# First weight differences of the second feed-forward block queued behind the last norm and the last sum; its operands transposed in another order

## The chip, the cores and the metric

One core of one Trainium2 chip runs the whole kernel. The metric is the device time of one execution in microseconds (us); a kernel's time is the median of its runs. Engines are named as in the profile: PE (TensorE matmuls), PEld (its weight loads), DVE (VectorE), ACT (ScalarE), POOL (GpSimd), SP (SyncE, whose queue issues the loads and stores).

## What is computed

One decoder layer on 1024 tokens of width 1024, in float32: a gated feed-forward half-step, a mixing stage (two kinds of attention, merged by gates), a second feed-forward half-step, and a gated per-layer embedding. The change lies where the mixing stage ends and the second feed-forward begins:

```python
def rms_norm(x, g):
    xf = x.astype(jnp.float32)
    r = lax.rsqrt(jnp.mean(xf * xf, axis=-1, keepdims=True) + NORM_EPS)
    return (xf * r).astype(x.dtype) * g

def swiglu(u, w_in, w_out):                      # w_in: 1024 x 5632, w_out: 2816 x 1024
    a, b = jnp.split(u @ w_in, 2, axis=-1)
    return (jax.nn.silu(a) * b) @ w_out
...
        h = h + merged @ w_out[i]
        h = h + FFN_RES_WEIGHT * swiglu(rms_norm(h, ffn2_norm[i]), ffn2_w_in[i], ffn2_w_out[i])
```

## The kernel before

**Products.** Each float32 operand is split into a high part (a cast to fp32r on ACT) and a low part (operand minus high part, on DVE or POOL); a product takes three matmuls, high by high, high by low, low by high.

**Tokens.** The residual stream h lies as eight tiles of 128 tokens, t = 0 to 7. `chunked` ends the mixing stage: for each t it adds the last product to h (two halves, line 256, DVE) and calls `after2(t)`, which stores h to DRAM, normalises it (`normed`: squares and their sum on ACT, line 303; the scale r on POOL, lines 201 and 202; h times r times the gain on DVE, line 305) and, for t from 4 on, calls `left.sums`.

**Seven products for eight.** The up-projection of the feed-forward works on a 2 by 2 block scheme with seven products per column block f of 128 hidden channels (22 blocks). Its left operands are seven sets, made from the normalised tokens: a11, a12 and a22 are quarters of them, s1 to s4 sums and differences of quarters, which `Left.sums` computes on POOL: for each of four token tiles the lines 330 (s1), 331 (s3), 333 (s2) and 334 (s4). `Left.put(name)` makes a set usable: for each of four tiles, four transposes on PE into one PSUM bank (line 187), a cast on ACT (line 211), a subtraction on DVE (line 212). A product (line 407) is 12 matmuls of 512 columns over all four tiles of one set. Its second matmul already reads low parts, so it needs the last tile's subtraction.

**Weights.** `load_a(f)` loads and splits the first weight tile (line 364, then 368 on ACT and 369 on POOL). `load_t(f)` loads the second, makes four differences on DVE (lines 384 to 387, two SBUF inputs each) and splits them: lines 368 (ACT) and 369 (POOL), twice for 128x1024 of differences and once for 128x512 of the raw tile ("wb"). A raw buffer is one of three; the next load into it waits for line 387 or for the splits.

**Order.** `Up.run` interleaves the first two column blocks: products 1 of block 0, 1 of block 1, 2 and 2, and then 5, 6, 7, 3, 4 of block 0 and the same of block 1. In `A_OF`, product 1 uses a11, 2 a12, 5 s1, 6 s2, 7 s3, 3 s4, 4 a22. After the n-th product one set of the list `puts` is put, and a hook for n is called: here `load_t(0)` at n = 1 and `load_t(1)` at n = 5. PE executes in the order of the code; the other engines' queues are ordered by a scheduler at build time, which may move instructions ahead of where the code has them. Every queue then runs strictly in that order.

Of the kernel before, what the change touches and what calls it, by code (L numbers as in the profile page):

```python
# [16 lines left out]
ALU = mybir.AluOpType  # L17
# [29 lines left out]
def hybrid_layer_kernel(  # L47
# [6 lines left out]
    nc = tc.nc  # L54
# [115 lines left out]
    def defer(ns, key, fn):  # L170
        later.append((pe["t"] + ns, key, fn))
        later.sort(key=lambda e: e[0])

    def need(key):

        mine = [e for e in later if e[1] == key]
        for e in mine:
            later.remove(e)
        for e in mine:
            e[2]()  # L180
# [14 lines left out]
    def rsqrt_mean(ss, n, cols=1, add=None):  # L195
        r = small.tile([P, 8], F32, tag="r", name="r")
        if add is not None:
            nc.gpsimd.tensor_scalar(r[:, :cols], ss, add, 1.0 / n, op0=ALU.add, op1=ALU.mult)
            nc.gpsimd.tensor_scalar(r[:, :cols], r[:, :cols], EPS, None, op0=ALU.add)
        else:  # L200
            nc.gpsimd.tensor_scalar(r[:, :cols], ss, 1.0 / n, EPS, op0=ALU.mult, op1=ALU.add)  # L201
        nc.gpsimd.tensor_tensor(r[:, :cols], r[:, :cols], mhalf[:, :cols], op=ALU.pow)
        return r

    def bcast_row(pool, v, n):
        g = pool.tile([P, n], F32, tag="gbc", name="gbc", bufs=1)
        nc.sync.dma_start(out=g[:, :n], in_=v.partition_broadcast(P))
        return g
# [92 lines left out]
    def normed(un, squares, src, g):  # L301
        ss = small.tile([P, 8], F32, tag="ss", name="ss")
        nc.scalar.activation(squares, src, AF.Square, accum_out=ss[:, 0:1])
        r = rsqrt_mean(ss[:, 0:1], DM)
        nc.vector.scalar_tensor_tensor(un, src, r[:, 0:1], g, op0=ALU.mult, op1=ALU.mult)

    class Left:

# [16 lines left out]
        def sums(self, t, part=(0, 1)):  # L325
            x11, x12 = self.un0[:, t, :512], self.un0[:, t, 512:]
            x21, x22 = self.un1[:, t, :512], self.un1[:, t, 512:]
            s1 = self.s1(t)
            if 0 in part:
                nc.gpsimd.tensor_add(s1, x21, x22)  # L330
                nc.gpsimd.tensor_sub(x21, x11, x21)
            if 1 in part:
                nc.gpsimd.tensor_sub(x11, s1, x11)
                nc.gpsimd.tensor_sub(self.s4(t), x12, x11)

        def put(self, name, ts=range(4)):
            pss = []
# [12 lines left out]
    class Up:  # L350
# [122 lines left out]
        def run(self, left, puts, late, hooks):  # L473

            two = [self.block(f, left) for f in range(2)]
            seq = [(0, 1), (1, 1), (0, 2), (1, 2)] + [(b, i) for b in range(2) for i in (5, 6, 7, 3, 4)]
            hooks = hooks | {6: lambda: self.load_a(2), 9: lambda: self.load_t(2)}
            for n, (b, i) in enumerate(seq):
                two[b][i]()
                if puts:  # L480
                    left.put(puts.pop(0))
                if n in hooks:
                    hooks[n]()
            for f in range(2, NF):
                b = self.block(f, left)
                b[1]()
                if f + 1 < NF:
                    self.load_a(f + 1)
                    self.load_t(f + 1)
                else:  # L490
                    late()
                for i in (6, 2, 5, 7, 3, 4) if f + 1 == NF else (6, 5, 2, 7, 3, 4):
                    b[i]()

    class Down:
# [73 lines left out]
        def run(self, scale, open_raws, open_norm, h_of, after):  # L569
# [36 lines left out]
            for n, (k, i) in enumerate(self.steps):  # L606
# [14 lines left out]
                if i == self.N - 1:  # L621
                    for j, ps in enumerate(pss.pop(k)):
# [7 lines left out]
    up = Up(ffn1_w_in, hs_d)  # L630
# [8 lines left out]
    left1 = Left(un0, un1, lambda t: s1_[t], lambda t: un0[:, t, 512:],  # L639
                 dict(a11=(upool, "u"), a12=(upool, "u"), a22=(upool, "u"), s3=(upool, "u"),  # L640
                      s1=(ux, "ux"), s2=(ux, "ux"), s4=(ux, "ux")))
# [41 lines left out]
    for t0 in range(0, NT, 2):  # L683
# [3 lines left out]
        r = rsqrt_mean(ss[:, :2], DM, 2)  # L687
# [7 lines left out]
    for c in range(2):  # L695
        col = slice(c * 512, (c + 1) * 512)
        for t in range(NT):
# [7 lines left out]
            n = c * NT + t  # L705
# [12 lines left out]
        for i in range(2):  # L718
            down.load(1, i, nc.gpsimd)

    up.run(left1, ["s1", "s2", "a22", "s3", "s4"], early, {1: open1, 4: lambda: up.load_t(1)})
    st_f.close()
    st_u.close()

    def run_down(down, name, h_src, gain, spill):

        st_h, st_n, st_r, st = (ExitStack() for _ in range(4))
        hp = phase(st_h, "h" + name, 1, "right")
        u, box = [], {}

        def open_raws(d):
            d.raws = phase(st_r, "raws" + name, 4, "right")
            d.more = phase(st, "dmore" + name, 1)
            d.temps = phase(st, "temps" + name)

        def h_of():
            h = box["h"] = hp.tile([P, NT, DM], F32, name="h")
            for t in range(NT):
                nc.sync.dma_start(out=h[:, t, :], in_=h_src[t * P:(t + 1) * P, :])
            return h  # L740

        def open_norm():
            st_r.close()
            box["n"] = phase(st_n, "norm" + name, 1, "right")
            box["g"] = bcast_row(box["n"], gain, DM)

        def after(t):
            if t % 4 == 0:
                u.append(new_u())
            norm_tile(box["n"], u, box["h"], t, box["g"], 7000.0 + 3200.0 * (t % 4))  # L750
            if spill:
                nc.sync.dma_start(out=h_spill[t * P:(t + 1) * P, :], in_=box["h"][:, t, :])

        down.run(0.5, open_raws, open_norm, h_of, after)
        st.close()
        return box["h"], u, (st_n, st_h)

    h, um, st_h = run_down(down, "1", x, mix_norm, True)
# [53 lines left out]
    left = [16 * 48 * 216.0]  # L812
# [189 lines left out]
    for t in range(NT):  # L1002
# [15 lines left out]
        r = rsqrt_mean(ss, QK, H)  # L1018
# [23 lines left out]
    for t in range(NT):  # L1042
# [15 lines left out]
        r = rsqrt_mean(ss, QK, H, add=sskr[:, t:t + 1])  # L1058
# [216 lines left out]
    h = hp.tile([P, NT, DM], F32, name="h2")  # L1275
# [24 lines left out]
        return hid  # L1300

    up = Up(ffn2_w_in, hs_d)
    left2 = []

    def ahead():
        up.load_a(0)
# [6 lines left out]
    def after2(t):  # L1313
        nc.sync.dma_start(out=h_spill[t * P:(t + 1) * P, :], in_=h[:, t, :])
        left = left2[0]
        un = (left.un0 if t < 4 else left.un1)[:, t % 4]
        normed(un, un, h[:, t, :], g2)
        if t < 4:
            defer(9500.0, "a11", lambda: left.put("a11", [t]))
        else:  # L1320
            if t == 5:
                need("a11")
                left.sums(0, (1,))
            left.sums(t - 4, (0,) if t == 4 else (0, 1))

    g2 = bcast_row(mp, ffn2_norm, DM)
    chunked(h, KT, (lambda ct: branch_w(w_branch_mla, ct), merge_up), w_out, 1.0, ahead,
            tuple(range(NT)), after2)
    need("a11")
    st.close()  # L1330
# [10 lines left out]
    def early2():  # L1341
        for i in range(2):
            down.load(1, i, nc.gpsimd)

    up.run(left2[0], ["a12", "s1", "s2", "s3", "s4", "a22"], early2,
           {1: lambda: up.load_t(0), 5: lambda: up.load_t(1)})
    st_f.close()
    st_u.close()
    h, u3, st_h = run_down(down, "2", h_spill, ple_norm, False)
# [4 lines left out]
    for c in range(2):  # L1354
        col = slice(c * 512, (c + 1) * 512)
        dg = [w_rows(w_ple_gate, 2 * j * P, c * 512, 512, 2) for j in range(4)]
        for half in range(2):
            need((id(u3), half))
            pss, pps = [bank() for _ in range(4)], []
            for k0 in (0, 4):  # L1360
                for j in range(4):
                    t, tc0 = 4 * half + j, j * P
# [47 lines left out]
```

## Time and profile before

| | |
|---|---|
| time, median of 3 runs (lowest, highest) | 2375.73 us (2372.26, 2380.26) |
| the profiled execution: its time, its span | 2373.98 us, 2371.9 us |
| PE busy | 2292.8 us, 97% of the span |
| DVE busy | 1525.5 us, 64% |
| ACT busy | 956.2 us, 40% |
| POOL busy | 852.1 us, 36% |
| chain that ended last, PE's share | 79% |

The busy share of an engine is an average over the span. PE is at work nearly all the time, so time can be lost or won where PE waits. The time of the profiled execution is 2.1 us longer than its span. Times below are us from the span's start.

### The profile page before, as it was taken

The numbers are of one execution on the slowest core, as the hardware profiler recorded it, in microseconds if no ns is written. First come the engines' busy times: TensorE is split into PE (matmuls) and PEld (weight loads), VectorE is DVE, ScalarE is ACT, GpSimd is POOL, SyncE is SP. The second block draws the span as 40 slices with busy tenths as digits, with TensorE's granted clock in tenths as the row PEclk, the third lists the DMA queues.
The fourth block names the chain that finished last, engine by engine and source line by source line (L and its number), as shares of the span: only waits on it lengthen the run. The fifth ranks groups of instructions, "written<-read, shape, count | busy, mean of one in ns | idle before, by whom it ended". The sixth has DMA issues, their size and how long they took to land.

```text
span 2371.9 us, 30099 instructions
## 1 busy us (share of the span) xinstructions
PE 2292.8 (97%) x11160; PEld 1912.0 (81%) x11160; DVE 1525.5 (64%) x2001; ACT 956.2 (40%) x1604; POOL 852.1 (36%) x654
## 2 busy tenths in 40 slices
PE   7899999999999999899999998998999999999999
PEld 6788888878888988777777887887888888888887
DVE  7667676657772224577777778557776666677842
ACT  5333233325452233455556666224233233244441
POOL 7444444400032233442333542547444444300030
PEclk9999999999999999999999999999999999999999
DMA  6223233385555324885453566512233332585432
GB/s 230 85 89 111 89 111 95 119 322 180 186 174 150 96 85 116 234 219 107 101 104 96 148 180 197 188 63 80 88 122 94 110 111 89 200 287 187 139 133 80
DMA packets 293890, 331.85 MB, mean 140 GB/s; under 512 B 16624, under 2 KB 200176, under 8 KB 293744
## 3 DMA queue, kind: packets, MB, share of 16 engines
q1 hardware_dynamic: 269808, 296.38, 39.0%
q0 software_dynamic: 23936, 33.56, 6.8%
q8 instruction: 87, 1.43, 0.2%
q14 instruction: 59, 0.48, 0.1%
HBM read 230.79 MB, written 99.09 MB: 139 GB/s over the span
## 4 chain that ended last, share of the span: by engine, by line
PE 79%; DVE 7%; DMA 5%; POOL 4%; issue 2%; ACT 2%; SPq 0%; DVEq 0%; ACTq 0%; POOLq 0%
PE T L183 37%; PE T L407 34%; PE A L183 5%; PE T L187 4%; DMA raw<-in_ffn_w_out_dram 2%; DVE D L1162 1%; POOL D L143 1%; DMA k_d<-ev 1%; DVE p L1162 1%; DVE D L1163 1%; DVE pt L212 1%; POOL D L369 1%; POOL hid L263 0%; DVE op L1112 0%; DMA un<-in_x_dram 0%
## 5 line engine op out<-in xcount | busy, mean ns | idle before, releaser
L407 PE MATMUL T<-u,D 128*128 128x512 f32 x3168 | 733.3, 391 | 3.6 <-DVE u L430 2.4
L407 PEld LDWEIGHTS T<-u,D 128*128 128x128 f32 x3168 | 596.0, 189 | 129.3 <-DVE u L430 4.1
L183 PE MATMUL T<-D 128*128 128x512 f32 x1944 | 452.4, 393 | 5.9 <-DVE u L212 2.3
L183 PEld LDWEIGHTS T<-D 128*128 128x128 f32 x1944 | 366.2, 189 | 83.5 <-ACT D L532 3.2
L369 POOL TENSOR_TENSOR D<-ts,D 128x1024 fp32r<-128x1024 f32 x88 | 216.5, 2460 | 309.9 <-ACT D L368 309.8
L183 PE MATMUL T<-u,D 128*128 128x512 f32 x1152 | 288.2, 396 | 11.1 <-DVE op L1112 11.1
L143 POOL TENSOR_TENSOR D<-raw,D 128x256 fp32r<-128x256 f32 (+6 forms) x159 | 188.4, 1211 | 292.2 <-ACT D L139 269.4
L183 PEld LDWEIGHTS T<-u,D 128*128 128x128 f32 x1152 | 209.2, 188 | 55.0 <-DVE op L1112 16.2
L532 ACT CAST D<-raw 128x512 fp32r<-128x512 f32 (+1 forms) x154 | 123.7, 807 | 225.2 <-PE T L183 113.7
L368 ACT CAST D<-ts 128x1024 fp32r<-128x1024 f32 x88 | 92.5, 1051 | 289.7 <-PE T L407 273.2
L201 POOL TENSOR_SCALAR r<-ss 128x1 f32<-128x1 f32 (+2 forms) x52 | 17.4, 335 | 497.7 <-ACT un L221 404.2
L183 PE MATMUL T<-D,u 128*128 128x512 f32 (+2 forms) x960 | 195.9, 362 | 0.0
L183 PEld LDWEIGHTS T<-D,u 128*128 128x128 f32 x960 | 166.2, 188 | 21.8
L533 DVE TENSOR_TENSOR D<-raw,D 128x512 fp32r<-128x512 f32 (+1 forms) x146 | 131.1, 900 | 60.3 <-ACT D L532 59.3
L212 DVE TENSOR_TENSOR pt<-T,pt 128x512 fp32r<-128x512 f32 (+1 forms) x160 | 101.1, 634 | 72.7 <-ACT pt L211 71.2
L369 POOL TENSOR_TENSOR D<-raw,D 128x1024 fp32r<-128x1024 f32 x44 | 121.2, 2756 | 34.1 <-ACT D L368 34.1
L407 PE MATMUL T<-u,wb 128*128 128x512 f32 x528 | 126.8, 389 | 0.0
L211 ACT CAST pt<-T 128x512 fp32r<-128x512 f32 (+1 forms) x160 | 86.7, 544 | 90.1 <-PE T L187 88.2
L384 DVE TENSOR_TENSOR ts<-raw 128x512 f32<-128x512 f32 x44 | 36.0, 818 | 134.6 <-POOL D L369 130.0
L407 PEld LDWEIGHTS T<-u,wb 128*128 128x128 f32 x528 | 99.1, 188 | 20.6
L385 DVE TENSOR_TENSOR ts<-raw,ts 128x512 f32<-128x512 f32 x44 | 114.1, 2594 | 0.0
L450 DVE TENSOR_TENSOR hidf<-u,sg 128x512 f32<-128x512 f32 x44 | 105.3, 2394 | 9.9 <-ACT sg L448 9.4
(224 smaller groups left out, 3311.6 us busy)
## 6 DMA issues: line engine op xcount, KB each, us to landing
raw<-in_ffn_w_in_dram SPq DMA_DIRECT2D x88, 512.0 KB, 3.9
raw<-hs_d SPq DMA_DIRECT2D x154, 256.0 KB, 2.7
hs_d<-hidf SPq DMA_DIRECT2D x110, 256.0 KB, 2.2
raw<-in_ffn_w_out_dram SPq DMA_DIRECT2D x110, 256.0 KB, 3.2
raw<-in_w_in_dram SPq DMA_DIRECT2D x28, 512.0 KB, 4.4
raw<-in_ffn_w_out_dram SPq DMA_DIRECT2D x22, 512.0 KB, 6.0
h_spill<-h SPq DMA_DIRECT2D x16, 512.0 KB, 3.0
gate_d<-gate SPq DMA_DIRECT2D x16, 512.0 KB, 2.9
```

The lines of the kernel that those rows point to most:

```text
L143: nc.gpsimd.tensor_sub(d[:, LO, c], raw[:, c], d[:, HI, c].bitcast(F32))
L183: nc.tensor.matmul(ps, lhs, rhs, start=start, stop=stop)
L187: nc.tensor.transpose(ps, src, ident)
L211: nc.scalar.copy(hi, ps)
L212: nc.vector.tensor_sub(lo, ps, hi.bitcast(F32))
L368: nc.scalar.copy(d[:, HI], src)
L369: nc.gpsimd.tensor_sub(d[:, LO], src, d[:, HI].bitcast(F32))
L385: nc.vector.tensor_sub(ts[:, 1], b22, ts[:, 0])
L407: nc.tensor.matmul(ps, b[:, l, k], a[:, r, k], start=start and k == n == 0, stop=k == 3 and n == 2, skip_group_check=True)
L450: nc.vector.tensor_mul(t["hid"][:, 512:], u3, sg)
L532: nc.scalar.copy(d[:, HI, cols], src)
L533: eng.tensor_sub(d[:, LO, cols], src, d[:, HI, cols].bitcast(F32))
```

## The change

Three things. `load_t(0)` of the second feed-forward runs under `tc.issue_after` for two instructions, the norm of t = 7 (line 305) and the last difference of `sums` for it (line 334): in DVE's queue its four differences stand behind that norm, and in POOL's queue its three splits stand behind that difference. Its instructions on ACT and its load are not bound. The list of sets becomes a12 after product n = 0, nothing after n = 1 and 2, then s1, s2, s3, s4, a22 after n = 3 to 7. And `load_t(1)` is called at n = 4. The first feed-forward's list is written in the new form and stays as it was.

```diff
@@ normed
-        nc.vector.scalar_tensor_tensor(un, src, r[:, 0:1], g, op0=ALU.mult, op1=ALU.mult)
+        return nc.vector.scalar_tensor_tensor(un, src, r[:, 0:1], g, op0=ALU.mult, op1=ALU.mult)
@@ Left.sums
-                nc.gpsimd.tensor_sub(self.s4(t), x12, x11)
+                return nc.gpsimd.tensor_sub(self.s4(t), x12, x11)
@@ Up.run
                 if puts:
-                    left.put(puts.pop(0))
+                    for name in puts.pop(0):
+                        left.put(name)
@@ after2
-        normed(un, un, h[:, t, :], g2)
+        n = normed(un, un, h[:, t, :], g2)
...
-            left.sums(t - 4, (0,) if t == 4 else (0, 1))
+            s = left.sums(t - 4, (0,) if t == 4 else (0, 1))
+            last[:] = [n, s]
@@ second feed-forward
-    up.run(left2[0], ["a12", "s1", "s2", "s3", "s4", "a22"], early2,
-           {1: lambda: up.load_t(0), 5: lambda: up.load_t(1)})
+    def first_t():
+
+        with tc.issue_after(last[0].ins), tc.issue_after(last[1].ins):
+            up.load_t(0)
+
+    up.run(left2[0], [["a12"], [], [], ["s1"], ["s2"], ["s3"], ["s4"], ["a22"]], early2,
+           {1: first_t, 4: lambda: up.load_t(1)})
```

PE, from the first product of the second feed-forward on, before (u_13645 is the set a11, u_13923 a12, u_13967 s1, u_14026 s2, u_14069 s3, u_14113 s4; un and s_13546 are what is transposed):

```order
L407 MATMUL T<-u_13645,D 128x512 x12
L187 MATMUL T<-ident,un 128x128 x16
L407 MATMUL T<-u_13645,D 128x512 x12
L187 MATMUL T<-ident,s_13546 128x128 x16
L407 MATMUL T<-u_13923,D 128x512 x12
L187 MATMUL T<-ident,un 128x128 x16
L407 MATMUL T<-u_13923,D 128x512 x12
L187 MATMUL T<-ident,un 128x128 x16
L407 MATMUL T<-u_13967,D 128x512 x12
L187 MATMUL T<-ident,s_13546 128x128 x16
L407 MATMUL T<-u_14026,D 128x512 x12
```

and now, after the second product (u_13923 is a12, u_14011 s1, u_14055 s2, u_14115 s3, u_14158 s4, u_14207 a22):

```order
L407 MATMUL T<-u_13923,D 128x512 x24
L187 MATMUL T<-ident,s_13546 128x128 x16
L407 MATMUL T<-u_14011,D 128x512 x12
L187 MATMUL T<-ident,un 128x128 x16
L407 MATMUL T<-u_14055,D 128x512 x12
L187 MATMUL T<-ident,un 128x128 x16
L407 MATMUL T<-u_14115,D 128x512 x12
L187 MATMUL T<-ident,s_13546 128x128 x16
L407 MATMUL T<-u_14158,wb 128x512 x12
L187 MATMUL T<-ident,un 128x128 x16
L407 MATMUL T<-u_14207,D 128x512 x12
```

Before, two products stood between the transposes of s1 and the product that reads it, and of the later sets too; now each of the sets s1 to a22 is transposed right ahead of its own product.

DVE, from the norm of t = 5 on, before (ts are the weight differences, T a PSUM bank):

```order
L305 SCALAR_TENSOR_TENSOR un<-h_12878,r,gbc 128x1024
L256 TENSOR_TENSOR h_12878<-T,h_12878 128x512 x2
L384 TENSOR_TENSOR ts<-raw 128x512
L386 TENSOR_TENSOR ts<-raw 128x512
L385 TENSOR_TENSOR ts<-raw,ts 128x512
L256 TENSOR_TENSOR h_12878<-T,h_12878 128x512
L387 TENSOR_TENSOR ts<-ts,raw 128x512
L305 SCALAR_TENSOR_TENSOR un<-h_12878,r,gbc 128x1024
```

behind which the four differences of block 1, the norm of t = 7 and the subtractions of a12, s1 and s2 follow; and now:

```order
L305 SCALAR_TENSOR_TENSOR un<-h_12878,r,gbc 128x1024 x2
L384 TENSOR_TENSOR ts<-raw 128x512
L386 TENSOR_TENSOR ts<-raw 128x512
L385 TENSOR_TENSOR ts<-raw,ts 128x512
L212 TENSOR_TENSOR u_13923<-T,u_13923 128x4x128 x3
L387 TENSOR_TENSOR ts<-ts,raw 128x512
L212 TENSOR_TENSOR u_13923<-T,u_13923 128x4x128
L384 TENSOR_TENSOR ts<-raw 128x512
L386 TENSOR_TENSOR ts<-raw 128x512
L385 TENSOR_TENSOR ts<-raw,ts 128x512
L387 TENSOR_TENSOR ts<-ts,raw 128x512
L212 TENSOR_TENSOR u_14011<-T,u_14011 128x4x128 x4
```

The norms of t = 6 and 7 now stand ahead of all eight differences; the differences of block 0 stand among the subtractions of a12, those of block 1 ahead of the subtractions of s1. In POOL's queue the splits of `load_t(0)` likewise stand behind all sums.

ACT, from the squares of t = 5 to 7 on, now (p copies a first product out, sg is the gate's activation):

```order
L303 ACTIVATE un,ss<-h_12878 128x1024 x3
L415 COPY p_13901<-T 128x512
L211 CAST u_13923<-T 128x4x128 x4
L368 CAST wb<-raw 128x512
L415 COPY p_13945<-T 128x512
L368 CAST D<-ts 128x1024 x2
L368 CAST wb<-raw 128x512
L420 ACT_TABLE_LOAD
L420 ACTIVATE sg<-T 128x512
L368 CAST D<-ts 128x1024
L420 ACTIVATE sg<-T 128x512
L368 CAST D<-ts 128x1024
```

Behind this piece stand the casts of s1. Before, the first two of them stood directly behind the casts of a12; now all weight casts of blocks 0 and 1 stand between.

## Rows read from the trace of the kernel before

**Rows 1.** Timeline of PE (start us, us, operation, count, [idle before]).

```profile
1605.26 12.54 PE L183 MATMUL T<-D,hid 128*128 128x512 f32 x54
...
1624.85 1.03 PE L187 MATMUL T<-ident,s 128*128 128x128 f32 x8
1636.12 2.04 PE L187 MATMUL T<-ident,s 128*128 128x128 f32 x8 [10.24 <-DVE u L212]
1637.82 4.67 PE L407 MATMUL T<-u,D 128*128 128x512 f32 x12
1642.33 1.91 PE L187 MATMUL T<-ident,un 128*128 128x128 f32 x16
...
1646.82 1.91 PE L187 MATMUL T<-ident,un 128*128 128x128 f32 x16
1648.48 2.98 PE L407 MATMUL T<-u,D 128*128 128x512 f32 x12
1651.30 1.91 PE L187 MATMUL T<-ident,s 128*128 128x128 f32 x16
...
1655.79 1.91 PE L187 MATMUL T<-ident,un 128*128 128x128 f32 x16
```

**Rows 2.** Timeline of ACT, same columns.

```profile
1619.86 1.05 ACT L303 ACTIVATE un<-h 128x1024 f32<-128x1024 f32 x1
...
1634.66 3.03 ACT L211 CAST u<-T 128x512 fp32r<-128x512 f32 x6 [3.85 <-DMA raw<-in_ffn_w_in_dram]
...
1653.24 2.06 ACT L211 CAST u<-T 128x512 fp32r<-128x512 f32 x4 [1.16 <-PE T L187]
```

**Rows 3.** Timeline of DVE, same columns.

```profile
1611.93 1.28 DVE L305 SCALAR_TENSOR_TENSOR un<-h,r,gbc 128x1024 f32<-128x1024 f32 x1 [1.56 <-POOL r L202]
...
1618.73 0.68 DVE L256 TENSOR_TENSOR h<-T,h 128x512 f32<-128x512 f32 x1
...
1624.64 1.70 DVE L384 TENSOR_TENSOR ts<-raw 128x512 f32<-128x512 f32 x1 [0.27 <-DMA raw<-in_ffn_w_in_dram]
...
1631.28 3.35 DVE L305 SCALAR_TENSOR_TENSOR un<-h,r,gbc 128x1024 f32<-128x1024 f32 x1
...
1644.58 2.48 DVE L212 TENSOR_TENSOR u<-T,u 128x512 fp32r<-128x512 f32 x4 [4.04 <-ACT u L211]
1647.01 0.69 DVE L384 TENSOR_TENSOR ts<-raw 128x512 f32<-128x512 f32 x1
...
1653.87 2.48 DVE L212 TENSOR_TENSOR u<-T,u 128x512 fp32r<-128x512 f32 x4 [0.35 <-ACT u L211]
...
1658.35 2.48 DVE L212 TENSOR_TENSOR u<-T,u 128x512 fp32r<-128x512 f32 x4 [1.41 <-ACT u L211]
```

**Rows 4.** Timeline of POOL, same columns.

```profile
1611.35 0.55 POOL L202 TENSOR_TENSOR r<-r,mhalf 128x1 f32<-128x1 f32 x1
...
1614.67 1.30 POOL L331 TENSOR_TENSOR un<-un 128x512 f32<-128x512 f32 x1
...
1624.50 1.28 POOL L330 TENSOR_TENSOR s<-un 128x512 f32<-128x512 f32 x1
...
1630.89 2.66 POOL L369 TENSOR_TENSOR D<-ts,D 128x1024 fp32r<-128x1024 f32 x1
...
1657.11 2.39 POOL L369 TENSOR_TENSOR D<-ts,D 128x1024 fp32r<-128x1024 f32 x1 [5.94 <-ACT D L368]
```

**Rows 5.** Chain of waits, a weight load of `load_t`, issue to landing (start us, us, what).

```profile
1631.42 3.25 DMA raw<-in_ffn_w_in_dram
```

**Rows 6.** Timeline of PE near the kernel's start.

```profile
26.33 4.61 PE L183 MATMUL T<-D 128*128 128x512 f32 x12 [2.33 <-DVE u L212]
```

**Rows 7.** Windows of 4 us: the stretch, its length, busy us by engine, PEclk, DMA share, GB/s.

```profile
24.00:28.00 4.00, 1.67 (x6) 1.39 (x6) 4.00 (x7) 3.29 (x6) 3.28 (x3) 0.86 0.85 285
```

**Rows 8.** PE's waits from 1665 to the end (waited for: us in total, times, longest).

```profile
PE T L407 <- DVE u L430: 0.8, 1, 0.8
PE T L183 <- DVE D L533: 0.8, 1, 0.8
```

More of the change, by code (lines that the diff above doesn't have):

```diff
@@ L719, in early @@
             down.load(1, i, nc.gpsimd)
-    up.run(left1, ["s1", "s2", "a22", "s3", "s4"], early, {1: open1, 4: lambda: up.load_t(1)})
+    up.run(left1, [[name] for name in ("s1", "s2", "a22", "s3", "s4")], early, {1: open1, 4: lambda: up.load_t(1)})
     st_f.close()
@@ L1302, in hybrid_layer_kernel @@
     up = Up(ffn2_w_in, hs_d)
-    left2 = []
+    left2, last = [], []
     def ahead():
```

## The prediction

> **What bounds the kernel now.** I read the timeline of PE first, since PE is busy for 97% of the span: only where it waits can time be won or lost. At the place of the change it has one long wait: eight of the sixteen transposes of s1 run at 1624.85, and the other eight start at 1636.12 after 10.24 us without work [rows 1]. The clock then costs more: these eight take 2.04 us where the first eight took 1.03, and the next product takes 4.67 where an undisturbed one takes 2.98 [rows 1], together 2.7. So the stretch holds 12.9 us that could go. Behind it PE waits only twice more up to the end, 0.8 us each [rows 8], so whatever is lost or won here reaches the end undiminished.
>
> What ends the wait? The transposes need a PSUM bank, and the banks are held by a12, whose casts start on ACT only at 1634.66 [rows 2]. The row names a load as what ended ACT's wait (landed at 1634.67, [rows 5]), but these casts read no raw buffer. At 1634.63 the norm of t = 7 ended on DVE (1631.28 plus 3.35, [rows 3]); a12's tile takes over memory that the norm's operands leave, so the casts wait for that norm. It is late because DVE first makes eight weight differences, and because DVE and POOL hold each other up: a difference takes 0.69 alone but 1.70 when it starts while POOL computes a sum (1624.50 plus 1.28 is 1625.78, and the difference ends 0.56 later) [rows 3, 4]; the norm takes 1.28 alone and 3.35 behind a split of 2.66 [rows 3, 4]. I read from this that a DVE instruction with two SBUF inputs and a POOL instruction exclude each other and take turns. The subtractions (line 212), which read PSUM, run at 2.48 for four throughout [rows 3].
>
> **Part 1: norm and sums first.** Now no difference stands ahead of the last norm. PE's last matmuls of h end at 1617.8 (1605.26 plus 12.54, [rows 1]); the add (0.68, [rows 3]) ends at 1618.5, the squares (1.05, [rows 2]) with their read-out at 1619.7. POOL, free at 1615.97 [rows 4], has by its order scale, sum, power and sum of the earlier tiles (0.2, 1.3, 0.55, 1.3), to 1619.5; then the norm of t = 6 takes its turn, to 1620.8; then scale 0.2, a sum 1.3, power 0.55, to 1622.8; the next sum, already queued, gets the turn, to 1624.1; the last norm ends at 1625.3, 9.3 us earlier than before. So far the change does what it says.
>
> But PE needs a12's last subtraction, and three differences stand ahead of the subtractions and the fourth ahead of the last one. They meet POOL's remaining sums, and by turns each costs 1.3 plus 0.6: three of them end at 1631.0. Three subtractions (1.86) end at 1632.9, the fourth difference waits once more, to 1633.7, the last subtraction ends at 1634.3. PE, through with its second product at 1624.85, waits until then: **9.4 us**, against 10.24. The bounds: if POOL never held DVE up, norm to 1624.0, differences to 1626.1, subtractions and the fourth difference, a12 would be ready at 1629.2, a wait of 4.3. I take 9.4, since every such difference in this stretch shows the hold-up. The slow clock after the wait is taken as before, 2.7.
>
> The Trainium skill (SBUF — State Buffer, section on who interferes with whom) says that a DVE instruction with two SBUF inputs and a GpSimd instruction that reads SBUF block each other for the whole instruction, and that issue order decides who blocks. The trace agrees (1.70 against 0.69). By this rule the lower bound of 4.3 is out and the 9.4 stands.
>
> **Part 2: the second load and ACT's queue.** `load_t(1)` needs the buffer that the fourth difference of block 0 frees, at 1633.7; its load takes 3.25 [rows 5], to 1637.0. POOL has finished the sums at 1635.0 and started on the splits, 2.39 each for 1024 columns [rows 4], the first to 1637.4. The four differences of block 1 now take turns with splits of 2.4, 1.3 and 1.3: 0.6 each with these between, to 1644.8. ACT's queue has two casts of these differences ahead of the casts of s1. The last of them (1.05, as the squares of the same size) ends at 1645.9, and from the first cast of a set to the last subtraction takes 3.1 (1653.24 to 1656.35, [rows 2, 3]): s1 is ready at 1649.0. PE, from 1634.3 on, does two products at 2.82 (start to start, [rows 1]), 1.66 for transposes (1646.82 to 1648.48) and loses 2.7 to the clock: 1644.3. It waits **4.7 us** for s1. Lower bound, by the undisturbed chain (load from 1628.6, four differences 2.8, cast 1.05, 3.1): s1 at 1638.8 against PE at 1636.5, so 2.3.
>
> **Part 3: transposes right ahead of their products.** Before, every set had a whole product and more between its transposes and its use. From the start of the transposes to the last subtraction a set took 4.73 (1642.33 to 1647.06), 5.05 (1651.30 to 1656.35) and 5.04 (1655.79 to 1660.83) [rows 1, 3], and nobody noticed, because a product and the next transposes lay between. Now the product follows at once, 1.66 after the transposes start, and its second matmul reads low parts. With 4.9 as the mean, PE waits 3.3 for each of s2, s3, s4 and a22: **13.1 us**. Floor: first tile's transposes 0.48, one cast 0.51, four subtractions 2.48, less 1.66, is 1.8 each, 7.2 in all. I take 13.1; weight casts and differences still stand between these conversions in the new order.
>
> **Part 4: the clock behind the new waits.** A wait of 2.33 us at 24.0 was followed by a product of 4.61 [rows 6], with the clock at 1.2 GHz for part of the stretch (0.86 granted in the mean, [rows 7]). Part 2 and 3 add five waits of this length or more. Between none and all five cost 1.7 each (4.67 less 2.98): 0 to 8.5. I take two, **3.4**, since some of the lost clock falls into the next wait.
>
> Free edits: the returned instructions and the list's form cost nothing. The splits of `load_t(0)` on POOL are now behind all sums, ready at 1637.4 and later, but product 5 wants them at 1644 or later; if the waits above were gone they would be next, since the sums alone end at 1635.0. SP's queue keeps its order; its loads move with the differences. In the down-projection a few splits and adds change places on DVE, near the second 0.8 wait [rows 8]: plus or minus 0.8.
>
> **Sum.** After: 9.4 + 2.7 + 4.7 + 13.1 + 3.4 = 33.3. Before: 12.9. Difference +20.4; 2373.98 (the profiled execution) + 20.4 = 2394.4. That execution is 1.75 below the median of the runs, less than their spread, so I leave it: **2394 us**.
>
> **Rivals.**
>
> *Faster: the conversions are covered.* If ACT and DVE kept up with the transposes, so that a set is ready when its transposes end, parts 2 and 3 cost nothing, and with undisturbed differences only 4.3 is left: 4.3 - 12.9 = -8.6, 2365 us. It decides at a lag of 1.66 from first transpose to last subtraction. For it: the long wait's cause, the late norm, is really removed. Against it: the lag is 4.7 to 5.05, and four subtractions alone take 2.48. 5%.
>
> *Little changes.* All at the lower bounds: 4.3 + 2.3 + 7.2 = 13.8, no slow clock, +0.9: 2375 us; with one of the bounds missed by some us, up to 2381. It holds if DVE is not held up by POOL. For it: the norm of t = 5 ran undisturbed (1.28). Against it: the rows of the hold-up. 12%.
>
> *Slow clock each time.* All five waits are followed by a slow product: 29.9 + 8.5 - 12.9 = +25.5, 2399.5 us. For it: the row at 26.33. Against it: part of the slow time would fall into waits. 18%. The Trainium skill (TensorE: Matmul & The Clock Gate, on how the oscillation bites) describes a kernel that waits at each tile and pays for the fall to half rate at each. That speaks for this rival; the trace of before has no such series.
>
> *The release does not work as said:* if a12's casts really waited for the load that the row names, the norm's 9.3 us would bring nothing; the wait would end with a load released at 1633.7, so about 1637.0 plus 3.1 for conversion, 5.8 later than forecast in part 1, while part 2 shrinks by as much (s1 is set by the differences). 2394 again; it changes no chance.
>
> **Chances and range.** The forecast, 2382 to 2397 (parts 1 to 3 each some us off), has 65%. A measurement of this kernel tells about 0.3% from no change, 7 us, so 2368.6 to 2382.9 counts as the same. Faster: 5%. Same: 12%, nearly all of the second rival. Slower: 83%. The range reaches from 2380, which leaves out the faster case and most of the second, to 2402, which takes in the third with the 0.8 and some us of spread.
>
> **What would show it.** In the timeline of PE: a wait of about 9 us ahead of the first product on a12, one of about 5 ahead of product 5, and four of about 3 behind the transposes of s2, s3, s4 and a22, each ended by a subtraction of line 212. On DVE the last norm ends near 1625. PEclk dips behind the waits. I am wrong if DVE's differences run at 0.7 beside POOL's sums, if a set is ready within 3 us of its first transpose, or if PE's idle time between 1615 and 1700 is not above 20 us.

## The result, and the profile after

The changed kernel takes **2394.24 us** (median of 4 runs, 2392.19 to 2398.68) against 2375.11 of the kernel before (median of 4, 2372.26 to 2380.26): ratio **1.0083**, 95% interval 1.0071 to 1.0095. It is slower by 19 us. The profiled execution took 2394.33 us and its span is 2392.6 us, 20.7 longer than the span before.

To find the place, I take one stretch of PE's timeline in both kernels: from the first product of the second feed-forward (line 407) to the product of block 1 that waits 0.8 us for a buffer (line 430). It holds the same matmuls in both. Its first and last row before:

```profile
1617.63 2.89 PE L407 MATMUL T<-u,D 128*128 128x512 f32 x12
...
1672.10 3.06 PE L407 MATMUL T<-u,D 128*128 128x512 f32 x12 [0.79 <-DVE u L430]
```

and its main rows after (timeline of PE: start us, us, operation, count, [idle before <- what ended it]; these rows answer to [rows 1]):

```profile
1616.41 2.88 PE L407 MATMUL T<-u,D 128*128 128x512 f32 x12
...
1620.80 2.98 PE L407 MATMUL T<-u,D 128*128 128x512 f32 x12
1625.67 0.49 PE L407 MATMUL T<-u,D 128*128 128x512 f32 x1 [1.89 <-ACT u L211]
1632.19 7.66 PE L407 MATMUL T<-u,D 128*128 128x512 f32 x23 [6.03 <-DVE u L212]
1639.69 1.91 PE L187 MATMUL T<-ident,s 128*128 128x128 f32 x16
1645.77 0.50 PE L407 MATMUL T<-u,D 128*128 128x512 f32 x1 [4.17 <-ACT u L211]
1646.83 4.37 PE L407 MATMUL T<-u,D 128*128 128x512 f32 x11 [0.56 <-DVE u L212]
1651.03 1.91 PE L187 MATMUL T<-ident,un 128*128 128x128 f32 x16
...
1656.08 4.11 PE L407 MATMUL T<-u,D 128*128 128x512 f32 x11 [1.76 <-DVE u L212]
1659.98 2.24 PE L187 MATMUL T<-ident,un 128*128 128x128 f32 x16
...
1664.33 2.81 PE L407 MATMUL T<-u,D 128*128 128x512 f32 x11 [0.56 <-DVE u L212]
1666.98 1.91 PE L187 MATMUL T<-ident,s 128*128 128x128 f32 x16
...
1672.08 5.06 PE L407 MATMUL T<-u,wb 128*128 128x512 f32 x11 [0.26 <-DVE u L212]
1676.94 2.29 PE L187 MATMUL T<-ident,un 128*128 128x128 f32 x16
...
1682.43 8.22 PE L407 MATMUL T<-u,D 128*128 128x512 f32 x35 [0.55 <-DVE u L212]
1691.44 3.02 PE L407 MATMUL T<-u,D 128*128 128x512 f32 x12 [0.79 <-DVE u L430]
```

The stretch, from the start of its first row to the start of its last, is 54.47 us long before and 75.03 after: **+20.56** of the 20.7. (It starts 1.22 earlier, less than the scatter of the stages ahead of it: in the nine profiles of this document it starts between 1613.98 and 1620.21. Behind it 1.36 is lost.) A pattern repeats five times: 16 transposes of a set, one matmul of its product, which needs high parts only, a wait, and the other eleven. Each time a conversion ends the wait: the cast (line 211) for the first matmul, the subtraction (line 212) for the second. No row names a transfer.

On DVE, the last norm, the differences of block 0 among the subtractions of a12, then those of block 1 ahead of s1's subtractions (answering to [rows 3]):

```profile
1621.17 2.31 DVE L305 SCALAR_TENSOR_TENSOR un<-h,r,gbc 128x1024 f32<-128x1024 f32 x1 [1.95 <-POOL r L202]
1623.41 1.75 DVE L384 TENSOR_TENSOR ts<-raw 128x512 f32<-128x512 f32 x1
1625.09 1.76 DVE L386 TENSOR_TENSOR ts<-raw 128x512 f32<-128x512 f32 x1
1626.77 1.74 DVE L385 TENSOR_TENSOR ts<-raw,ts 128x512 f32<-128x512 f32 x1
...
1630.23 1.30 DVE L387 TENSOR_TENSOR ts<-ts,raw 128x512 f32<-128x512 f32 x1
1631.46 0.68 DVE L212 TENSOR_TENSOR u<-T,u 128x512 fp32r<-128x512 f32 x1
1635.27 2.60 DVE L384 TENSOR_TENSOR ts<-raw 128x512 f32<-128x512 f32 x1 [3.14 <-DMA raw<-in_ffn_w_in_dram]
...
1644.28 2.48 DVE L212 TENSOR_TENSOR u<-T,u 128x512 fp32r<-128x512 f32 x4 [2.30 <-ACT u L211]
```

The sums on POOL beside them (answering to [rows 4]):

```profile
1624.58 1.71 POOL L330 TENSOR_TENSOR s<-un 128x512 f32<-128x512 f32 x1
1626.26 1.70 POOL L334 TENSOR_TENSOR s<-un 128x512 f32<-128x512 f32 x1
```

And on ACT the casts of a12, the last weight cast ahead of s1, and the casts of s1 (answering to [rows 2]):

```profile
1623.56 2.05 ACT L211 CAST u<-T 128x512 fp32r<-128x512 f32 x4 [3.64 <-DVE un L305]
...
1642.73 1.03 ACT L368 CAST D<-ts 128x1024 fp32r<-128x1024 f32 x1
1643.66 2.05 ACT L211 CAST u<-T 128x512 fp32r<-128x512 f32 x4
```

The last norm ends at 1623.48, and a12's casts start 0.08 later. Before, they started at 1634.66 [rows 2]. So that half of the change works: the cause of the old wait is gone 11 us earlier. But a12's last subtraction ends only at 1632.14, 8.66 after the norm, since all four differences stand ahead of it and DVE and POOL go in step: a difference starts every 1.68 us (1623.41, 1625.09, 1626.77), and so does a sum (1624.58, 1626.26).

The clock, in windows of 4 us (columns as in [rows 7]; the number behind POOL's busy time is the granted clock, 1.00 for 2.4 GHz and 0.50 for 1.2 GHz):

```profile
1662.00:1666.00 4.00, 2.40 (x11) 1.60 (x9) 2.27 (x4) 1.22 (x3) 1.72 (x1) 1.00 0.02 4
1672.00:1676.00 4.00, 3.92 (x9) 3.14 (x10) 0.02 (x1) 0.00 (x0) 0.00 (x0) 0.50 0.00 0
```

In the second of these the eleven matmuls from 1672.08 take 5.06 us; from 1664.33, at the full clock, eleven take 2.81. From 1700 to the end PE waits twice (answering to [rows 8]): 0.8 us for line 534, which was line 533 before, and

```profile
PE T L183 <- ACT D L533: 0.9, 1, 0.9
```

This second one is new; it is most of the 1.36 lost behind the stretch.

### The profile page after: what moved, and what is told of

Same layout as the page of the kernel before. It is cut to its first block, busy times and chain, and to the rows that moved or that the text cites. A ratio compares the mean times of both kernels' runs of the same rounds, so it can differ in the third digit from the quotient of the medians.

```text
span 2392.6 us, 30095 instructions
## 1 busy us (share of the span) xinstructions
PE 2300.2 (96%) x11160; PEld 1914.6 (80%) x11160; DVE 1524.1 (64%) x2001; ACT 956.2 (40%) x1604; POOL 850.2 (36%) x654
## 4 chain that ended last, share of the span: by engine, by line
PE 78%; DVE 8%; DMA 6%; POOL 4%; issue 3%; ACT 2%; SPq 0%; DVEq 0%; ACTq 0%; POOLq 0%
PE T L183 36%; PE T L407 34%; PE A L183 4%; PE T L187 3%; DMA raw<-in_ffn_w_out_dram 2%; DVE D L1163 1%; POOL D L143 1%; DMA k_d<-ev 1%; DVE u L212 1%; DMA hd<-sbk_d 1%; DVE D L1164 1%; DVE p L1163 1%; POOL D L369 1%; DVE pt L212 1%; POOL hid L263 0%
## 5 line engine op out<-in xcount | busy, mean ns | idle before, releaser
L407 PE MATMUL T<-u,D 128*128 128x512 f32 x3168 | 737.5, 392 | 23.4 <-ACT u L211 10.1
L369 POOL TENSOR_TENSOR D<-raw,D 128x1024 fp32r<-128x1024 f32 x44 | 120.6, 2741 | 33.3 <-ACT D L368 33.3
```

Of the source, the lines that this page charges most:

```text
L369: nc.gpsimd.tensor_sub(d[:, LO], src, d[:, HI].bitcast(F32))
L407: nc.tensor.matmul(ps, b[:, l, k], a[:, r, k], start=start and k == n == 0, stop=k == 3 and n == 2, skip_group_check=True)
```

## The experiments

The theory under test is that of the prediction: the old wait goes, but a12 waits for differences that take turns with POOL's sums, s1 waits behind block 1's weight work, and the transposes that stand right ahead of their product show a conversion time that was covered before. The rivals: a12 waits for something else, such as a load; DVE and POOL do not take turns but share a bandwidth; the conversions are as late wherever the transposes stand. For each kernel the table has its time, the ratio against times of the kernel before that were taken together with it, and the stretch above in its profiled execution.

| kernel | time, us | ratio (95%) | stretch, us | against 54.47 |
|---|---|---|---|---|
| changed | 2394.24 | 1.0083 (1.0071, 1.0095) | 75.03 | +20.56 |
| binding alone | 2372.24 | 0.9995 (0.9986, 1.0003) | 51.88 | -2.59 |
| list alone | 2397.25 | 1.0096 (1.0083, 1.0110) | 78.49 | +24.02 |
| one product between | 2374.84 | 1.0002 (0.9993, 1.0011) | 55.67 | +1.20 |
| bound behind a12 | 2374.57 | 1.0000 (0.9991, 1.0010) | 54.95 | +0.48 |
| sums in halves | 2393.17 | 1.0085 (1.0072, 1.0099) | 74.54 | +20.07 |
| second load late | 2390.03 | 1.0070 (1.0057, 1.0083) | 70.99 | +16.52 |
| both | 2369.93 | 0.9988 (0.9979, 0.9997) | 50.49 | -3.98 |

Where times differ by some 3 us or less, the place is read from the stretch, since the stages ahead of it alone differ by up to 6 us between these profiles.

### The binding alone

```diff
-    up.run(left2[0], [["a12"], [], [], ["s1"], ["s2"], ["s3"], ["s4"], ["a22"]], early2,
-           {1: first_t, 4: lambda: up.load_t(1)})
+    up.run(left2[0], [["a12"], ["s1"], ["s2"], ["s3"], ["s4"], ["a22"]], early2,
+           {1: first_t, 5: lambda: up.load_t(1)})
```

> The changed kernel with the list of sets and the hook as before (a12, s1, s2, s3, s4, a22 after the first six products, load_t(1) after the sixth): the binding of load_t(0) alone. Theory (the loss comes from the list, the binding itself shortens the wait for a12): the last norm ends some 9 us earlier than before and PE's long wait shrinks from 10.2 to 5 to 6 us, since the subtractions of a12 still stand behind three differences; no wait of over 1 us ahead of the products on s1 to a22. Time 4 us below the kernel before, about 2371. Rival (the binding costs by itself, because the splits of the first weights come behind the sums): a wait ahead of product 5 of some us, time equal to the kernel before or up to 5 above it.

The long wait of 10.24 [rows 1] is 4.60 here, with two smaller ones behind it (PE's timeline):

```profile
1633.05 1.58 PE L187 MATMUL T<-ident,s 128*128 128x128 f32 x8 [4.60 <-DVE u L212]
...
1636.01 4.91 PE L407 MATMUL T<-u,D 128*128 128x512 f32 x11 [0.95 <-DVE u L212]
...
1657.42 3.00 PE L407 MATMUL T<-u,D 128*128 128x512 f32 x12 [1.20 <-ACT u L211]
```

The binding gains 2.6 us in the stretch, where 4 were expected; the time itself can't tell that from nothing. The slow product behind the wait stays (4.91), and the wait of 1.20 ahead of the product on s3 is one that was not expected. No wait stands ahead of product 5, the place that the rival named.

### The list alone

```diff
-           {1: first_t, 4: lambda: up.load_t(1)})
+           {1: lambda: up.load_t(0), 4: lambda: up.load_t(1)})
```

> The changed kernel without the binding: load_t(0) is free as before, the list of sets and the hook of load_t(1) are those of the change. Theory: PE's wait for a12 is as long as before (about 10 us, to the end of the late norm and a12's conversion), each of s1, s2, s3, s4, a22 is waited for by 2 to 3.5 us right behind its transposes, some products run slow behind these waits; about 20 us above the kernel before, 2395, so as slow as the full change. Rival (binding and list only cost together, since it is the bound weight differences that hold up the conversions): waits under 1 us behind the transposes and a time within 5 us of the kernel before.

The new list, with its hook at n = 4, costs 24.0 in the stretch without the binding and 23.2 with it (75.03 less 51.88); the binding gains 2.6 without the list and 3.5 with it. The two parts add up to within 0.9, and the list alone makes the loss. Two waits are longer than expected. PE waits 12.7 for a12, since the transposes of s1 no longer fill part of that time, and 7.1 for s1, here behind two weight differences of block 2 (on DVE, 1644.47 to 1648.97) beside a sum and a split on POOL:

```profile
1652.02 5.06 PE L407 MATMUL T<-u,D 128*128 128x512 f32 x11 [4.79 <-DVE u L212]
```

What releases a12's casts can be read here and in the other kernels. ACT's row names a load, as the one of before did [rows 2]:

```profile
1632.39 2.05 ACT L211 CAST u<-T 128x512 fp32r<-128x512 f32 x4 [3.85 <-DMA raw<-in_ffn_w_in_dram]
```

while DVE's row of the last norm reads

```profile
1629.00 3.36 DVE L305 SCALAR_TENSOR_TENSOR un<-h,r,gbc 128x1024 f32<-128x1024 f32 x1
```

The norm ends at 1632.36, and the casts start 0.03 later; the load lands at 1632.41, when they have started. Two events so close can't be told apart safely, and before they were as close (1634.63 and 1634.67). The changed kernel decides it: there the casts start 0.08 after the norm, whose name their row has, and the next load lands only at 1635.25, 11.7 later. The other kernels in which the norm comes early show the same lag, 0.07 to 0.08. It is the norm.

### One product between a set's transposes and its use

```diff
-    up.run(left2[0], [["a12"], [], [], ["s1"], ["s2"], ["s3"], ["s4"], ["a22"]], early2,
+    up.run(left2[0], [["a12"], [], ["s1"], ["s2"], ["s3"], ["s4"], ["a22"]], early2,
```

> The full change with one edit: s1 is put after the third product instead of the fourth, and s2 to a22 likewise one product earlier, so that one product lies between the transposes of a set and its use. Theory: the four waits for s2 to a22 (12.4 us together) and the slow products behind them are gone, the wait for s1 shrinks to 1 or 2 us; 20 us below the full change, 2372 to 2375. Rival (the conversions are late because of ACT's and DVE's queues, whatever lies between): waits of 2 us or more remain ahead of products 5 to 4, time 2382 or more.

One product more between takes back 19.4 of the 20.6 us. The waits for s1 to a22 are now 0.5, 1.2, 0.8, 0 and 0.4 (measured as in the table below; the 0.8 is for a buffer, line 430). The wait for a12 stays, and the clock behind it:

```profile
1631.43 5.06 PE L407 MATMUL T<-u,D 128*128 128x512 f32 x11 [6.02 <-DVE u L212]
```

The conversions are no shorter than before (a22 takes 5.0 from its first transpose at 1657.21 to its last subtraction); they lie beside a product and the next set's transposes now, 4.5 us from start to start together. This is what part 3 rests on, and its rival (the conversions are late whatever lies between) is out.

### The differences bound behind a12's last subtraction

As the kernel above, and `first_t` binds on DVE to the subtraction that completes a12 instead of the last norm:

```diff
-        with tc.issue_after(last[0].ins), tc.issue_after(last[1].ins):
+        with tc.issue_after(left2[0].last.ins), tc.issue_after(last[1].ins):
```

(`put` stores the subtraction of line 212 in `left.last`.)

> As the kernel with one product ahead, and the differences of load_t(0) are bound on DVE behind the last subtraction of a12 instead of behind the last norm. Theory (three differences by turns with POOL's sums delay a12 by 5 to 6 us): a12 is ready 3.2 us after the last norm, PE waits 3 to 3.5 us for it, with little or no slow clock after it; then some 4 us for s1, whose casts stand behind both weight casts of block 0 on ACT; 2367 to 2370, below the kernel before. Rival (the wait for a12 is ended by something else, a load or a bank): the wait stays at 8 us or more and the time at that of the kernel with one product ahead.

This missed. Its first half came as expected: the second matmul on a12 starts at 1629.88, 2.9 later than it would without a wait, against 8.3 in the kernel above. But of these 5.5 the stretch gains 0.7 (54.95 against 55.67). The wait for s1, expected at some 4, is 6.1 where it was 0.5, and a slow product stands behind each of the two waits (4.14 and 4.38 for eleven matmuls):

```profile
1629.88 4.14 PE L407 MATMUL T<-u,D 128*128 128x512 f32 x11 [0.55 <-DVE u L212]
...
1644.63 0.76 PE L407 MATMUL T<-u,D 128*128 128x512 f32 x1 [3.82 <-DVE u L212]
1646.33 4.38 PE L407 MATMUL T<-u,D 128*128 128x512 f32 x11 [0.94 <-DVE u L212]
```

On DVE, three of s1's four subtractions stand behind two differences of block 1, the first of the three at 1643.81, and the last behind a third difference; the differences take turns with POOL's splits:

```profile
1639.95 2.26 DVE L384 TENSOR_TENSOR ts<-raw 128x512 f32<-128x512 f32 x1
1642.13 1.75 DVE L386 TENSOR_TENSOR ts<-raw 128x512 f32<-128x512 f32 x1
```

So the differences are paid for by whichever set stands behind them. Two experiments go on from there: one tests the turns, the other takes block 1's weight work out from ahead of s1.

### The sums made in halves

The full change, with each sum of lines 330 to 334 as two POOL instructions of 256 columns, for instance:

```diff
-                nc.gpsimd.tensor_add(s1, x21, x22)
+                for c in (slice(0, 256), slice(256, 512)):
+                    nc.gpsimd.tensor_add(s1[:, c], x21[:, c], x22[:, c])
```

> The full change, but each of POOL's sums of 512 columns (lines 330 to 334) is made as two of 256. Theory: a DVE instruction with two SBUF inputs and a POOL instruction exclude each other and take turns, so a DVE difference beside a sum waits for the POOL instruction that is running, whatever its length. With sums half as long the differences 384, 386 and 385 beside them take 1.1 to 1.4 us instead of 1.75, a12's last subtraction ends 1 to 2 us sooner after the end of the last norm (8.7 us in the changed kernel), and the time is 2391 to 2394. Rival: both engines share the bandwidth of the port and nothing takes turns; then the length of POOL's instructions is no matter, the differences stay at 1.7 to 1.8, a12 is ready 8.7 us after the norm and the time stays at 2394.

The lines of the file shift by six here. DVE, the first two differences:

```profile
1627.19 1.21 DVE L390 TENSOR_TENSOR ts<-raw 128x512 f32<-128x512 f32 x1
1628.32 1.21 DVE L392 TENSOR_TENSOR ts<-raw 128x512 f32<-128x512 f32 x1
```

and POOL beside them:

```profile
1627.81 1.17 POOL L337 TENSOR_TENSOR un<-s,un 128x256 f32<-128x256 f32 x1
1628.94 1.18 POOL L332 TENSOR_TENSOR s<-un 128x256 f32<-128x256 f32 x1
```

Both engines now step every 1.13 us instead of 1.68. The work of a difference is the same; what it waits for is half as long. By the rival it would have stayed at 1.75. So they do take turns, instruction by instruction. The Trainium skill (SBUF — State Buffer, section Who interferes with whom) calls the shared port pair an exclusive lock, held for a whole instruction; the trace agrees, with steps of 1.68 and 1.13. Each step is some 0.3 shorter than the two instructions alone (0.69 and 1.29; 0.69 and 0.72), so a small part of them still overlaps.

a12 is ready 6.52 us after the last norm (1627.26) instead of 8.66, and still the time does not move: s1's second matmul starts some 23.4 us after the norm in both kernels, and PE waits longer for it. The first casts of s1 did come sooner, 18.2 after the norm instead of 20.2. But in this kernel's queue on ACT a weight cast that waited for its load (1.80) stands between the second and the third conversion of s1, where the changed kernel has it behind the fourth:

```profile
1645.46 1.07 ACT L211 CAST u<-T 128x512 fp32r<-128x512 f32 x2
1648.33 1.04 ACT L374 CAST D<-raw 128x1024 fp32r<-128x1024 f32 x1 [1.80 <-DMA raw<-in_ffn_w_in_dram]
1649.28 1.07 ACT L211 CAST u<-T 128x512 fp32r<-128x512 f32 x2
```

The theory was right on the mechanism and on the differences. Its time, 2391 to 2394, holds the 2393.17, but the ratio, 1.0085 against 1.0083, shows no gain at all, and it did not say that. What 2.1 us of an earlier a12 are worth without that weight cast in the way is not shown.

### The second load called later

The full change, with one number altered, so that s1's conversions stand ahead of block 1's casts and differences:

```diff
-           {1: first_t, 4: lambda: up.load_t(1)})
+           {1: first_t, 7: lambda: up.load_t(1)})
```

> The full change, but load_t(1) is called after product n = 7 and no longer after n = 4, so that on ACT and DVE the conversions of s1 stand ahead of block 1's weight casts and differences. Theory: PE waits for s1 because these casts and differences stand ahead of its conversions; the wait falls from 5.2 us to 2.1 to 2.5 (the conversion's own length less the transposes), the other waits stay within 1 us of what they are, and the time is about 3 lower, 2391. Rival: the wait for s1 is its own conversion and the release of its bank; it stays near 5 and the time at 2394.

```profile
1637.24 1.91 PE L187 MATMUL T<-ident,s 128*128 128x128 f32 x16
...
1641.08 2.81 PE L407 MATMUL T<-u,D 128*128 128x512 f32 x11 [0.55 <-DVE u L212]
...
1648.19 4.27 PE L407 MATMUL T<-u,D 128*128 128x512 f32 x11 [0.22 <-DVE u L212]
```

From the start of s1's transposes to the second matmul takes 3.84, of which 1.9 would pass without a wait: the wait is 1.9, where it was 5.2. The others add up to 12.2 (12.4 in the changed kernel). So s1 waited behind block 1's weights, and its own conversion is no slower than the others. The stretch is 4.0 shorter, 3.3 of it this wait; product 5 now runs at the full clock (2.81), and others do not (4.27 for product 6). The ratio falls by 0.0013, some 3 us; the two intervals overlap, so the gain is read from the stretch.

### Both orders put right

The sets in the order of before, the differences bound behind a12's last subtraction, and the late second load:

```diff
+        with tc.issue_after(left2[0].last.ins), tc.issue_after(last[1].ins):
+            up.load_t(0)
...
+    up.run(left2[0], [["a12"], ["s1"], ["s2"], ["s3"], ["s4"], ["a22"]], early2,
+           {1: first_t, 7: lambda: up.load_t(1)})
```

> Norm and sums first as in the change, but the sets in the order of before (a12, s1, s2, s3, s4, a22 after the first six products), the differences of load_t(0) bound on DVE behind a12's last subtraction instead of the last norm, and load_t(1) after n = 7. Theory: a12 is ready 3.2 us after the last norm; no wait of PE between 1615 and 1700 is above 3 us, together 2 to 3, and the slow clock hardly shows; the time is 2365 to 2367, some 8 below the kernel before. Rival: the weight splits of block 0, on POOL behind all sums and now later by the differences, are not ready when product 5 wants them; then PE waits 3 us or more ahead of product 5, the clock falls, and the time is 2370 or more.

2369.93 us against 2372.9 of the kernel before, taken together with it: ratio 0.9988, with an interval that ends below 1. It is faster than the kernel before, but by 3 us and not by 8, and faster than the changed kernel by some 23 (by the ratios). a12 is ready 3.2 after the last norm (1627.61 and 1624.43), as expected, and the wait of ten us is gone. What came in its place, on PE:

```profile
1638.68 2.58 PE L407 MATMUL T<-u,D 128*128 128x512 f32 x10 [1.52 <-POOL D L369]
...
1651.60 4.58 PE L407 MATMUL T<-u,D 128*128 128x512 f32 x12 [1.17 <-DVE u L430]
```

and on DVE ahead of the second of these

```profile
1641.37 2.52 DVE L384 TENSOR_TENSOR ts<-raw 128x512 f32<-128x512 f32 x1 [1.60 <-DMA raw<-in_ffn_w_in_dram]
```

Product 5 waits 1.5 for a split of block 0's weights: the rival was right on the place, and its price is half of what it said. Then the subtractions of the last sets stand behind this difference and the next (1.77), which take turns with splits: four waits of 0.5 to 1.2 from 1646 on, and a slow product. The seven waits of the stretch add up to 5.4 where 2 to 3 were expected.

## Why the prediction was right

Forecast 2394, measured 2394.2. That they agree to 0.2 us is in part luck: as a difference, 20.4 was forecast, and it is 19.1 between the medians and 20.7 between the two profiled spans. The steps, with what each term measured in the changed kernel (a wait is how much later the product's second matmul starts than it would without one: it follows 0.24 behind the product's start, or 1.9 behind the start of transposes right ahead of it):

| term | forecast | measured | rows |
|---|---|---|---|
| wait for a12 | 9.4 | 8.3 | 1632.19, without a wait 1623.86 |
| slow clock behind it | 2.7 | 2.2 | 7.66 for 23 matmuls, 5.4 undisturbed |
| wait for s1 | 4.7 | 5.2 | 1639.69 to 1646.83 |
| waits for s2, s3, s4, a22 | 13.1 | 12.4 | 3.15, 2.45, 3.2, 3.6 |
| slow clock behind these five | 3.4 | 5.8 | 4.37, 4.11, 5.06 for 2.81; 2.24, 2.29 for 1.91 |
| sum | 33.3 | 33.9 | |

Less the 12.9 of before the difference is 21.0 against 20.4 forecast, and 20.56 in the stretch. The half us between these can be the slow transposes: their 0.7 is counted in the last row and also lies inside a wait.

**The mechanism held at every step.** Part 1: the last norm was forecast to end 9.3 us earlier than before, and ends 11.15 earlier, 1.2 of which is the earlier start of the stretch. Differences beside sums were put at 1.9 each; they step by 1.68, and over three of them that takes 0.7 off the wait for a12. (That every difference of the stretch before shows the hold-up says too much: three of the eight took 0.68 to 0.71. Those that started while a sum or a split ran on POOL show it.) That POOL holds DVE up, the point on which the second rival hung, is shown by the sums in halves. Part 2: the load landed 3.65 after its issue (3.25 assumed), s1's casts stand behind block 1's last weight cast (1642.73 plus 1.03, casts at 1643.66), and from first cast to last subtraction it is 3.1 as forecast; moving the load away took 3.3 of 5.2 off. Part 3: four waits with a mean of 3.1 (3.3 forecast), and one product more between leaves 2.4 of their 12.4. The release is shown too: a12's casts follow the norm and not the load that the profile of the kernel before names.

**The size that was off** is the clock in part 4. Two slow products were assumed; three of the five are slow, and two sets of transposes besides, 5.8 instead of 3.4. That lies between the forecast and the rival that had all five slow (8.5). Smaller waits for a12 and the later sets made up for it, so the total agrees better than its terms: 1.1 and 0.5 and 0.7 too much, 0.5 and 2.4 too little. One further term was not in the sum but in the margin: a new wait of 0.9 for a cast in the down-projection.

**What was missed** lies in the experiments, twice at the same place. With a12 ready 5.5 us sooner (bound behind a12), or 2.1 sooner (halved sums), the wait for s1 grew by about as much. In the first the differences stand ahead of s1's subtractions instead: the eight must pass DVE somewhere, at 1.7 each beside POOL and 0.7 alone, and the set behind them pays. In the second it is a weight cast and its load, on ACT, among the conversions of s1.

## To carry to other kernels

Before you move a producer to just ahead of its consumer, read from the trace how long it takes from the first instruction to the last result; what lay between them before was cover. Here one product and the next set's transposes, 4.5 us together, take the waits for five sets from 17.6 us to 2.9. A queue binding that removes the cause of the longest wait gains only up to the next item that stands in the same queues (here 2.6 to 3.5 of 12.9 us): ask who is behind the moved work on each engine. When the profile names what ended a wait, compare the ends of all candidates; of two events 0.04 us apart the name can be the wrong one, and a kernel that moves them apart decides.

## What the runs showed of the hardware

- While both queues are full, DVE's weight differences (two SBUF inputs) and POOL's sums alternate one for one, and both engines step at one period: 1.68 us with sums of 512 columns, 1.13 with sums of 256. Halving the instructions of the one speeds up the other. Subtractions that read PSUM are not held up: in the changed kernel four take 2.48 beside POOL's splits (from 1644.28) and 2.48 while POOL does nothing (from 1669.54).
- Waits of nearly the same length are followed by a slow product or not. (A wait here has two idle times of PE with one matmul between, as in the rows above.) In the list alone the wait of 3.2 ahead of the product on s4 (idle 2.14 and 0.55) is followed by full speed and one of 3.2 ahead of the product on a22 (idle 2.14 and 0.55) by 9.87 us for 35 matmuls, where the changed kernel takes 8.22 behind its wait of 3.6; and in the kernel with the late second load a wait of 2.6 (s2) is followed by 4.27 for eleven, while one of 3.3 (s4) is followed by 2.79. The length of the wait alone does not decide it. In the four kernels that transpose right ahead of the product, seven of the fourteen waits between 2.4 and 3.6 us are followed by a slow product, which costs 1.3 to 2.3 us more. What does decide it was not settled here.
